# A recurrence with its inverse as products on quarters of the array, fewer half writes, six banks, and queues issued in a listed order

## The chip, the core and the metric

One core of a Trainium2 chip runs the whole program. The metric is the device time of one execution in microseconds (us), the median of several. The engines are TensorE (PE, with its weight loads as PEld), VectorE (DVE), ScalarE (ACT), GpSimd (POOL) and SyncE (SP), which issues the DMAs.

## What is computed

Two transformer blocks in sequence over 512 tokens of 1024 features, in float32 with a context of 256 tokens. The part that matters here is the scan of the second layer of the first block, over 16 heads of 64 features, in two directions, first over the context and then over the tokens:

```python
def step(S, inp):
    w_t, k_t, v_t, kk_t, kka_t = inp[:5]
    S = (S * w_t[:, :, None, :]
         - jnp.einsum('bhij,bhj->bhi', S, kk_t)[..., None] * kka_t[:, :, None, :]
         + v_t[..., None] * k_t[:, :, None, :])
    y = jnp.einsum('bhij,bhj->bhi', S, inp[5]) if emit else None
    return S, y
```

The decay `w_t` comes from a bias, `w0`, and a low-rank product, through a sigmoid and an exponential. What is read out of the scan (`rwkv_readout`) is normalised by head, given a bonus term and a gate, and multiplied by a weight.

## The kernel before

The kernel computes the scan in chunks of 64 tokens. `wkv` makes 24 cells, 3 rounds of 8: round `b` is the context for 0 and a half of the tokens for 1 and 2, and `p` is a pair of heads; both directions `d` of 4 chunks each are in one cell, so a tile of [128, 8, 64] holds 2 heads on the partitions and 8 chunks. Cell i needs the state `H` that cell i-8 left.

`cell` (line 1225) loads k, kk, r, the low-rank weights l2 and w0 (spread over 128 partitions on the host); forms the decay from T1 and l2 in PSUM, adds w0 on DVE, takes the Tanh on ACT; sums the decays with a triangular product (tri) and exponentiates them to W and iW; writes BC (each head's two operands side by side, so in halves of 64 partitions, on DVE and POOL), AQ and Qz. `intra` (line 1340) makes the scores of 64 by 64 tokens (SC), and inverts a triangular matrix per chunk and head: three levels and a correction, 18 products that depend on each other, each copied out of PSUM by ACT (`cp`) or masked by DVE. Its left operands MB, ML and GT lie in zeroed tiles `bd`, [128, 8, 2, 64] float16, with the two heads' blocks on the diagonal, so `bdm` is 8 products of 128 by 128 on the whole array:

```python
for e in range(8):
    mm(ps[:, e], L[:, e].rearrange("p h t -> p (h t)"), x[:, e], start=first and e == 0, stop=last and e == 7)
```

`plus` adds a tile by one product of 512 columns with an identity, and `tr` transposes with 16 products on quarters (64 by 64, one per head). Because of the zeros, what DVE writes into GT is written in two halves. `step` (line 1450), four times a cell, is the scan over chunks: X from SC and HV, copied to Xs by ACT; U from TTz and Xs, copied into HV, one half by ACT and one by DVE; HU from the identity, BCt and HV, scaled by DVE into the next HV; for the tokens also Q, added into ytm. `readout` (line 1512) normalises a pair of heads after round 2, with DVE, ACT and POOL.

PSUM has 4 banks `ps` for the inverse and the scores and 4 `ch` for the steps. At most three cells hold the tiles SC, BCt, TTz and HV. What sets the order: the cells and readouts are generators, which `Clock.weave` (line 96) runs by turns, each to its next yield, the lowest cell first among those that an estimate of the engines' times finds ready; signals such as ("chain", i - 3) keep a cell from starting early. The instructions so traced go to a scheduler behind it, which sorts each engine's queue by its own estimates. On the chip each queue is worked off in order. Every operation goes through one helper, so the profile shows line 176 for all of them; the tile names tell them apart (`bd` for MB, ML and GT, `f` for the float16 copies, `c_...` for constants).

Of the kernel before, what the change touches and what calls it, by code (L numbers as in the profile page):

```python
# [14 lines left out]
PSUM = bass.MemoryType.PSUM  # L15

P = 128
D = 1024
KD = 8
# [6 lines left out]
class Clock:  # L26
# [5 lines left out]
    def __init__(self):  # L32
        self.free, self.wrote, self.used = {}, {}, {}
        self.now = self.end = 0.0
        self.events = {}
        self.fresh = []
        self.taken = self.given = 0
        self.tiled = False

# [95 lines left out]

def _cost(eng, fn, out, ins, tiled=False):
    n = _size(out)
    if eng == "PE":
        if tiled and ins[0].dtype == F32 and min(ins[0].shape[0], _size(ins[0])) <= 64:

            return 0.5 * (0.00085 if fn == "transpose" else 0.0017) * max(n, 60)
# [12 lines left out]


class Engine:
# [5 lines left out]
    def __getattr__(self, fn):  # L162
        real, clock, eng = getattr(self._r, fn), self._c, self._n

        def call(*a, **k):
            aps = [x for x in list(a) + list(k.values()) if isinstance(x, bass.AP)]
            out = k.get("out", a[0] if a else None)
            ins = [x for x in aps if x is not out]
            outs = [out.tensor.name]
            if "accum_out" in k:  # L170
                outs.append(k["accum_out"].tensor.name)
            if eng == "DMA":
                clock.dma(outs[0], [x.tensor.name for x in ins], out.shape[0] * _size(out) * 4)
            else:
                clock.op(eng, _cost(eng, fn, out, ins, clock.tiled), outs, [x.tensor.name for x in ins])
            return real(*a, **k)  # L176

        setattr(self, fn, call)
        return call


# [7 lines left out]
class Core:  # L189
# [54 lines left out]
    def ring(self, pool, shape, tag, bufs, dt=F32):  # L244

        t = pool.tile(shape, dt, name=self.nm(tag), tag=tag, bufs=bufs)
        r = self.rings.setdefault((id(pool), tag), [])
        r.append(t.tensor.name)
        if len(r) > bufs:
            self.clock.follow(r[-1], r[-1 - bufs])  # L250
# [248 lines left out]
class First:  # L499
# [691 lines left out]
    def wkv(self, dr, ytm, bonus):  # L1191
# [3 lines left out]
        v, s, g = nc.vector, nc.scalar, nc.gpsimd  # L1195
        es = c.psums(ps=4, ch=4)
        c.clock.tiled = True
        self.op = pool = es.enter_context(c.tc.tile_pool(reuse_waits="tile", name="wkv", bufs=1))
        for n in ("id16", "a0", "ka", "rk", "scmask", "lvl", "tri", "i16", "iq", "hsel"):
            setattr(self, n, self.load_in(pool, n))  # L1200
# [18 lines left out]
        c.clock.tiled = False  # L1219
        es.close()  # L1220
# [4 lines left out]
    def cell(self, i, b, p, dr, ytm, bonus):  # L1225
# [32 lines left out]
        for j in range(2):  # L1258
            for d in range(2):
                mm(ps[d][:, j * P:(j + 1) * P], self.T1[rr[d], qd[d] * 256 + j * P:qd[d] * 256 + (j + 1) * P], l2[rr[d], :P], start=j == 0, stop=False)  # L1260
        for d in range(2):
            mm(ps[d][:, 256:], l2[rr[d], P:], self.A1[rr[d], tok[d]], start=False, stop=True)
        for d in range(2):
# [3 lines left out]
        yield  # L1267
        s.activation(sw, sw, AF.Tanh, scale=0.5)
        yield
# [19 lines left out]
        yield  # L1289
        BC, AQ = self.wt([8, 2, 64], "BC"), self.wt([8, 2, 64], "AQ")  # L1290
        v.scalar_tensor_tensor(th8, th8, 1.0, kk8, op0=ALU.add, op1=ALU.mult)
        for h in range(2):

            rr = np.s_[h * 64:(h + 1) * 64]
            v.scalar_tensor_tensor(BC[rr, :, h], th8[rr], 0.5, iW[rr], op0=ALU.mult, op1=ALU.mult)
            g.tensor_tensor(BC[rr, :, 1 - h], kd[rr], iW[rr], op=ALU.mult)
        a = AQ[:, :, 0]
# [42 lines left out]
    def intra(self, i, out, BC, AQ):  # L1340
# [9 lines left out]
        bc = lambda h, e: BC[hs[h], e].rearrange("p o s -> p (o s)")  # L1350
        SC = []
        for d in range(2):
            sc = self.wt([2, 4, P], "SC", 6)
            ps = [c.psum().rearrange("p (c t) -> p c t", c=4) for _ in range(2)]
            for ch in range(4):
                for h in range(2):
                    mm(ps[h][:, ch, :nq], bc(h, d * 4 + ch), AQ[hs[h], d * 4 + ch].rearrange("p o s -> p (o s)")[:, :nq], start=ch == 0, stop=ch == 3)
            for h in range(2):
                v.tensor_tensor(sc[:, h, :, :nq], ps[h][:, :, :nq], self.scmask[:, d, :nq].unsqueeze(1).to_broadcast([P, 4, nq]), op=ALU.mult)
                m = sc[hs[h], h, :, :64]  # L1360
                s.copy(MB[hs[h], d * 4:(d + 1) * 4, h], m)
                (g, v)[h].tensor_tensor(ML[hs[h], d * 4:(d + 1) * 4, h], m, MB[hs[h], d * 4:(d + 1) * 4, h], op=ALU.subtract)
                g.tensor_copy(m, AQ[hs[h], d * 4:(d + 1) * 4, 0])
# [3 lines left out]
        for e in range(8):  # L1367
            for h in range(2):
                nc.tensor.transpose(pt[h][:, e], bc(h, e), c.ident[hs[h], hs[h]])
        for h in range(2):  # L1370
            s.copy(BCt[:, :, h], pt[h])
# [78 lines left out]
    def step(self, p, qd, st, SC, BCt, TT, Qz, HV, wc, ytm):  # L1450
# [15 lines left out]
        s.copy(Xs, X)  # L1466
        HU = half()
        for d, h in DH:
            mm(HU[hs[h], d], c.ident[:, hs[h]], HV[:, es[d], h], start=d == 0, stop=False)
        if out:  # L1470

            Q = half()
            for h, d in DH:
                mm(Q[hs[d], h], Qz[:, es[d], h], HV[:, es[d], h], start=h == 0, stop=False)
        yield
# [6 lines left out]
        for d, h in DH:  # L1482
            mm(HU[hs[h], d], BCt[:, es[d], h], HV[:, es[d], h], start=False, stop=d == 1)
        if st < 3:
# [4 lines left out]
        if out:  # L1489
            for h, d in DH:  # L1490
                mm(Q[hs[d], h], SC[d][:, h, chs[d], 64:128], HV[:, es[d], h], start=False, stop=h == 1)
            for d in range(2):
# [19 lines left out]
    def readout(self, p, dr, y, bonus, ring, G1):  # L1512
# [19 lines left out]
        yield ("chain", 2 * KD + p)  # L1532
        sm = c.tmp.tile([P, 8], F32, name=c.nm("gs"), tag="gs")
        v.reduce_sum(sm, e8(y), axis=X1)
# [8 lines left out]
        yield  # L1543
        vr = c.tmp.tile([P, 8], F32, name=c.nm("gv"), tag="gv")
        v.reduce_sum(vr, e8(t), axis=X1)
# [10 lines left out]
        for j in range(4):  # L1556
            nc.tensor.transpose(pt[:, j * P:(j + 1) * P], y[:, j * P:(j + 1) * P], c.ident)
        s.copy(y, pt)
        yield
        ps = c.psum()  # L1560
        c.mm3(ps, (wh, wl), np.s_[:, :], G1, np.s_[:, :], True, True)
        v.tensor_tensor(y, y, ps, op=ALU.mult)
# [1057 lines left out]
```

## Time and profile before

| | |
|---|---|
| median of 3 runs | 4526.43 us (4525.61 to 4526.72) |
| profiled execution | 4529.56 us |
| its span, first to last instruction | 4527.8 us |
| mean granted clock of TensorE | 0.945 |
| busy in the span | PE 4146.5, DVE 2583.0, ACT 1747.0, POOL 1150.1 us |

The span is what the profile divides up; the time of the execution has 1.8 us more around it. A busy PE counts an instruction from its start to its modelled end, and consecutive products overlap. [...]

### The profile page before, as it was taken

What the parts mean: (1) busy time and instruction counts of PE and PEld (TensorE: products, weight loads), DVE (VectorE), ACT (ScalarE), POOL (GpSimd) and SP (SyncE); (2) the same over time, 40 slices, a digit from 0 to 9 for tenths busy, and PEclk for the clock granted to TensorE, in tenths of its full rate; (3) what the DMA queues carried; (4) which work ended last, traced back from release to release, by engine and by line L of the source; (5) the groups of instructions that cost most, each with busy time, mean ns of one, the idle gap of its engine ahead of it and who ended that gap; (6) DMA issues with size and microseconds to landing.
All of it is one profiled execution on the core that took longest, in us unless ns stands there. A gap on an engine that the chain in (4) does not pass through costs nothing. (4 is left out here: it accounts for less than half of the span.)

```text
span 4527.8 us, 69045 instructions
## 1 busy us (share of the span) xinstructions
PE 4146.5 (92%) x27872; PEld 3436.0 (76%) x27872; DVE 2583.0 (57%) x4105; ACT 1747.0 (39%) x3265; POOL 1150.1 (25%) x1122
## 2 busy tenths in 40 slices
PE   5897899997897988887999999988999999979998
PEld 4786688886685777766888788876888888857887
DVE  8998844345934666677644543486433433584333
ACT  4454422223534556544522432225322322334222
POOL 4223300003514344453200211163201201353111
PEclk8898999999898899988999999998999999979999
DMA  6444421212233111112432322220332323211332
GB/s 220 148 134 134 148 75 62 65 63 96 84 122 102 42 46 52 47 40 63 137 107 94 98 95 97 93 76 18 103 98 94 97 96 96 93 38 62 97 98 84
DMA packets 193889, 408.80 MB, mean 90 GB/s; under 512 B 46496, under 2 KB 87456, under 8 KB 193568
## 3 DMA queue, kind: packets, MB, share of 16 engines
q1 hardware_dynamic: 193568, 404.37, 27.8%
q8 instruction: 219, 3.59, 0.3%
q14 instruction: 102, 0.84, 0.1%
HBM read 386.47 MB, written 17.83 MB: 89 GB/s over the span
## 5 line engine op out<-in xcount | busy, mean ns | idle before, releaser
L176 PE MATMUL pj<-a,wh 128*128 128x512 f32 (+1 forms) x5328 | 1420.2, 356 | 73.7 <-DVE a L176 32.2
L176 PE MATMUL ps<-a,wh 128*128 128x512 f32 x4192 | 1293.4, 390 | 12.0 <-DVE a L176 6.4
L176 ACT CAST wh<-wr 128x1024 fp32r<-128x1024 f32 (+3 forms) x548 | 565.2, 1031 | 1643.9 <-PE ps L176 952.6
L176 PEld LDWEIGHTS pj<-a,wh 128*128 128x128 f32 x5328 | 951.6, 195 | 221.8 <-issue 43.7
L176 PE MATMUL pj<-a,wl 128*128 128x512 f32 (+1 forms) x2664 | 939.2, 353 | 26.5 <-DVE wl L176 20.5
L176 PEld LDWEIGHTS ps<-a,wh 128*128 128x128 f32 x4192 | 786.5, 188 | 176.9 <-DVE a L176 7.5
L176 PE MATMUL ps<-a,wl 128*128 128x512 f32 x2096 | 815.5, 389 | 0.0
L176 DVE TENSOR_TENSOR wl<-wr,wh 128x1024 fp32r<-128x1024 f32 (+3 forms) x490 | 599.1, 1223 | 301.9 <-ACT wh L176 269.7
L176 PEld LDWEIGHTS pj<-a,wl 128*128 128x128 f32 x2664 | 517.9, 195 | 102.2 <-DVE wl L176 26.7
L176 PEld LDWEIGHTS ps<-a,wl 128*128 128x128 f32 x2096 | 393.8, 188 | 81.8
L176 POOL TENSOR_TENSOR t<-t,a 128x512 f32<-128x512 f32 x94 | 159.6, 1699 | 1113.4 <-ACT t L176 1113.4
L176 POOL TENSOR_TENSOR a<-a,t 128x512 f32<-128x512 f32 (+1 forms) x109 | 142.1, 1306 | 1023.0 <-ACT t L176 1021.6
L176 PE MATMUL ps<-a,a 128*128 128x256 f32 (+4 forms) x859 | 195.7, 383 | 35.4 <-ACT a L176 15.1
L176 ACT CAST f<-ps 128x512 f16<-128x512 f32 x312 | 178.0, 587 | 119.9 <-PE ps L176 117.9
L176 DVE SCALAR_TENSOR_TENSOR ytm<-ps,ytm 128x512 f32<-128x512 f32 x96 | 66.4, 692 | 264.9 <-PE ps L176 264.9
L176 DVE TENSOR_TENSOR t<-t,ps 128x512 f32<-128x512 f32 x87 | 59.8, 688 | 275.2 <-PE ps L176 270.6
L176 DVE TENSOR_TENSOR a<-a,pj 128x512 f32<-128x512 f32 (+1 forms) x176 | 101.2, 578 | 166.9 <-PE pj L176 166.9
L176 PEld LDWEIGHTS <-bd 128*128 128x128 f16 x3264 | 139.8, 102 | 72.3 <-issue 24.7
L176 PEld LDWEIGHTS ps<-a,a 128*128 128x128 f32 (+1 forms) x859 | 136.2, 212 | 73.0 <-ACT a L176 24.3
L176 POOL TENSOR_TENSOR wl<-wr,wh 128x1024 fp32r<-128x1024 f32 x58 | 150.8, 2605 | 148.1 <-ACT wh L176 126.2
L176 DVE TENSOR_TENSOR t<-ps,a 128x512 f32<-128x512 f32 x86 | 59.2, 691 | 220.5 <-PE ps L176 220.5
L176 DVE SCALAR_TENSOR_TENSOR a<-a,c_cvw,a 128x511 f32<-128x511 f32 (+15 forms) x180 | 177.7, 1007 | 2.3
(301 smaller groups left out, 5557.7 us busy)
## 6 DMA issues: line engine op xcount, KB each, us to landing
wr<-in_f1w SPq DMA_DIRECT2D x120, 512.0 KB, 3.5
wr<-in_f2w SPq DMA_DIRECT2D x120, 512.0 KB, 3.5
ada<-in_adaT SPq DMA_DIRECT2D x88, 512.0 KB, 3.6
wr<-in_m0w SPq DMA_DIRECT2D x76, 512.0 KB, 3.6
wr<-in_m1w SPq DMA_DIRECT2D x76, 512.0 KB, 3.6
wr<-in_ev_o SPq DMA_DIRECT2D x16, 512.0 KB, 3.9
wr<-in_w_o SPq DMA_DIRECT2D x16, 512.0 KB, 3.5
k<-d_k SPq DMA_DIRECT2D x48, 128.0 KB, 2.2
```

The source lines that it names most:

```text
L176: return real(*a, **k)
```

## The change

The three masked operands become dense tiles of [128, 8, 64], and each whole-array product becomes two products on quarters, one per head; `plus` likewise. GT and RT are written once for all 128 partitions, and BC gets a layout with k's operand in the middle, shared by both heads' reads, so that POOL writes it once. w0 is loaded as one row per direction into a zeroed tile and added by a product with a tile `first`, which has ones in one row per direction, and ACT takes the Tanh from PSUM. The banks become 6 `ps`, 1 `ch` (X and U) and 1 `hq` (HU and Q). The generators are run one after the other into a `Plan`, which keeps every instruction as a step (consecutive PE instructions of a cell are one step), and lists them by a greedy simulation with a price for each and room for each ring of tiles; the four engines' queues then follow that list.

```diff
@@ Engine.__getattr__ @@
+            if clock.plan is not None:
+                return clock.plan.add(eng, fn, lambda: real(*a, **k), out, ins, outs)
@@ new: class Step (one instruction, or a group of PE's) @@
+    def product(self, fn, out, ins):
+        k, m, n = ins[0].shape[0], _size(ins[0]), _size(out)
...
+        mode = k > 64, m > 64
+        if self.mode is None:
+            self.first = mode
+        elif mode != self.mode:
+            self.at = self.cost + 0.1
...
+        once = max(0.00084 * n, 0.054) if plain else 0.00042 * n + 0.003
...
@@ new: class Plan @@
+    LAT = 0.2
+    def add(self, eng, fn, call, out, ins, outs):
+        st = self.steps[-1] if self.steps else None
+        if not (st and eng == st.eng == "PE" and st.rank[0] == self.rank):
+            st = Step(eng, outs[0], (self.rank, len(self.steps)))
+            self.steps.append(st)
...
+            if eng == "ACT":
+                st.cost = 0.17 + 0.00082 * n
+            elif eng == "DVE":
+                st.cost = 0.16 + 0.00105 * n
+            elif fn == "tensor_tensor":
+                st.cost = 0.2 + 0.0024 * n
+            else:
+                st.cost = 0.18 + 0.0009 * n
...
+    def order(self):
...
+                    t = max(f + (self.SWITCH if eng == "PE" and steps[i].first != mode else 0.0), ready[i])
+                    need = {}
+                    for x in uses[i]:
+                        if x not in held:
+                            need[self.place[x]] = need.get(self.place[x], 0) + 1
+                    for k, n in need.items():
+                        if len(room[k]) < n:
+                            break
+                        t = max(t, sorted(room[k])[n - 1] + 0.1)
+                    else:
+                        at[i] = t
...
+                lo = min(at.values())
+                i = min((x for x in at if at[x] <= lo + self.SLACK), key=lambda x: steps[x].rank)
+                if best is None or at[i] < best[0]:
+                    best = at[i], i
...
+        return [steps[i] for _, i in sorted(out)]
+    SWITCH = 0.1
+    SLACK = 0.1
@@ wkv @@
-        es = c.psums(ps=4, ch=4)
+        es = c.psums(ps=6, ch=1, hq=1)
...
-        self.bd = [[zero(pool.tile([P, 8, 2, 64], F16, name=c.nm("bd"))) for _ in range(3)] for _ in range(3)]
-        cells = [self.cell(i, i // KD, i % KD, dr, ytm, bonus) for i in range(3 * KD)]
+        self.w0z = [zero(pool.tile([P, P], F32, name=c.nm("w0z"))) for _ in range(3)]
+        self.first = zero(pool.tile([P, P], F32, name="first"))
...
-        c.clock.weave(cells + [self.readout(p, dr, ytm[p], bonus, ring, self.G1) for p in range(KD - 1)])
+        plan = c.clock.plan = Plan()
+        for i in range(3 * KD):
+            plan.rank = i
+            run(self.cell(i, i // KD, i % KD, dr, ytm, bonus))
+            if i >= 2 * KD and i < 3 * KD - 1:
+                plan.rank = i + 1.5
+                run(self.readout(i - 2 * KD, dr, ytm[i - 2 * KD], bonus, ring, self.G1))
+        c.clock.plan = None
+        with c.tc.manual_schedule(engines={E.PE, E.Activation, E.DVE, E.Pool}):
+            for step in plan.order():
+                for call in step.calls:
+                    call()
@@ cell @@
-        w0 = self.wt([2, P], "w0")
-        nc.sync.dma_start(w0, c.A["w0r"][:, :, p * P:(p + 1) * P])
+        w0 = self.w0z[i % 3]
+        for d in range(2):
+            nc.sync.dma_start(w0[d * 64:d * 64 + 1], c.A["w0r"][0:1, d, p * P:(p + 1) * P])
...
+        for j in range(2):
+            for d in range(2):
+                mm(ps[d][:, j * P:(j + 1) * P], self.first[rr[d]], w0[rr[d]], start=False, stop=False)
...
-            v.tensor_tensor(sw[:, 2 * d:2 * d + 2], ps[d][:, :256].rearrange("p (j f) -> p j f", j=2),
-                            w0[:, d].unsqueeze(1).to_broadcast([P, 2, P]), op=ALU.add)
+            s.activation(sw[:, 2 * d:2 * d + 2], ps[d][:, :256].rearrange("p (j f) -> p j f", j=2), AF.Tanh, scale=0.5)
...
-        s.activation(sw, sw, AF.Tanh, scale=0.5)
...
-            g.tensor_tensor(BC[rr, :, 1 - h], kd[rr], iW[rr], op=ALU.mult)
+        g.tensor_tensor(BC[:, :, 1], kd, iW, op=ALU.mult)
@@ intra @@
-        MB, ML, GT = self.bd[i % 3]
+        MB, ML, GT = (self.wt([8, 64], n, 3, F16) for n in ("MB", "ML", "GT"))
...
-                mm(ps[:, e], L[:, e].rearrange("p h t -> p (h t)"), x[:, e], start=first and e == 0, stop=last and e == 7)
+                for h in range(2):
+                    mm(ps[hs[h], e], L[hs[h], e], x[hs[h], e], start=first and e == 0, stop=last and e == 7)
...
-            mm(ps.rearrange("p e t -> p (e t)"), self.id16, x.rearrange("p e t -> p (e t)"), start=True, stop=False)
+            for h in range(2):
+                mm(ps[hs[h]].rearrange("p e t -> p (e t)"), self.i16[hs[h]], x[hs[h]].rearrange("p e t -> p (e t)"), start=True, stop=False)
...
-            for h in range(2):
-                v.tensor_tensor(GT[hs[h], :, h].rearrange("p (d c) t -> p d c t", d=2), ps[hs[h]].rearrange("p (d c) t -> p d c t", d=2),
-                                self.lvl[hs[h], l].unsqueeze(2).to_broadcast([64, 2, 4, 64]), op=ALU.mult)
+            v.tensor_tensor(GT.rearrange("p (d c) t -> p d c t", d=2), ps.rearrange("p (d c) t -> p d c t", d=2),
+                            self.lvl[:, l].unsqueeze(2).to_broadcast([P, 2, 4, 64]), op=ALU.mult)
...
-        for h in range(2):
-            v.tensor_tensor(RT[hs[h], :, h], iq[hs[h]], ps[hs[h]], op=ALU.subtract)
+        v.tensor_tensor(RT, iq, ps, op=ALU.subtract)
@@ step @@
-        HU = half()
+        HQ = c.bank("hq", (P, 2, 2, 64))
+        HU, Q = HQ[:, 0], HQ[:, 1]
```

The readouts' small tiles become rings of two, and its gate products are issued before ACT's copy.

## Rows read from the trace of the kernel before

**Rows 1.** Stretches: us, busy PE PEld DVE ACT POOL (count), clock, DMA share, GB/s.

```profile
1406.00:2128.00 722.00, 621.28 (x10513) 506.44 (x10513) 491.12 (x950) 403.56 (x925) 314.55 (x451) 0.89 0.17 47
1660.00:1880.00 220.00, 195.02 (x3677) 159.90 (x3676) 151.10 (x288) 140.72 (x344) 96.88 (x141) 0.96 0.17 48
1880.00:2110.00 230.00, 195.31 (x3173) 159.63 (x3173) 166.45 (x332) 108.39 (x242) 106.21 (x129) 0.84 0.13 36
```

**Rows 2.** The same view, middle stretch, instructions on H alone (DVE, POOL).

```profile
1660.00:1880.00 220.00, 2.33 (x8) 4.60 (x16) 0.96 0.17 48
```

**Rows 3.** Waits of PE in the recurrence: us in total, times, longest.

```profile
PE ch L176 <- DVE hv L176: 29.3, 24, 3.6
```

**Rows 4.** Timeline of DVE: start, us, what; idle before and what ended it.

```profile
2094.57 0.69 DVE L176 TENSOR_TENSOR ytm<-ytm,gv 128x512 f32<-128x512 f32 x1 [1.76 <-POOL gv L176]
2095.30 1.39 DVE L176 TENSOR_TENSOR bd<-ps,c_lvl 64x512 f16<-64x512 f32 x2
2096.72 0.69 DVE L176 TENSOR_TENSOR ytm<-ytm,ps 128x512 f32<-128x512 f32 x1
2097.44 0.29 DVE L176 COPY hv<-ch 64x128 f32<-64x128 f32 x1
```

**Rows 5.** Two stretches, one at each clock (columns as in the first group).

```profile
1444.00:1491.00 47.00, 39.36 (x770) 31.31 (x766) 30.56 (x56) 31.39 (x69) 16.05 (x28) 1.00 0.12 32
1492.00:1502.00 10.00, 9.94 (x110) 8.49 (x111) 6.45 (x13) 3.73 (x10) 1.54 (x3) 0.51 0.13 38
```

**Rows 6.** The same stretches, PE's whole-array products (those that read bd) alone.

```profile
1444.00:1491.00 47.00, 15.49 (x328) 1.00 0.12 32
1492.00:1502.00 10.00, 1.67 (x24) 0.51 0.13 38
```

**Rows 7.** Timeline of PE at the upper clock.

```profile
1673.27 1.61 PE L176 MATMUL ps<-AQ,BC 64*128 64x128 f32 x16
1674.80 0.45 PE L176 MATMUL ch<-Xs,TTz 128*64 128x64 f32 x8
...
1680.42 0.40 PE L176 MATMUL ch<-hv,c_ident 128*64 128x64 f32 x8
1680.65 0.40 PE L176 MATMUL ch<-hv,Qz 128*64 128x64 f32 x8
1680.98 0.44 PE L176 MATMUL ps<-c_i,f 64*64 64x64 f16 x16
1681.35 0.45 PE L176 MATMUL ch<-Xs,TTz 128*64 128x64 f32 x8
1681.73 0.39 PE L176 MATMUL ps<-c_iq,c_id 128*128 128x512 f16 x1
1681.96 0.40 PE L176 MATMUL ps<-c_iq,bd 128*128 128x64 f16 x8
1682.19 0.38 PE L176 MATMUL ps<-f,c_id 128*128 128x512 f16 x1
```

**Rows 8.** Timeline of PE at the lower clock.

```profile
1492.06 0.60 PE L176 MATMUL ps<-c_i,f 64*64 64x64 f16 x16 [0.92 <-ACT f L176]
1492.59 1.97 PE L176 MATMUL ps<-AQ,BC 64*128 64x64 f32 x16
...
1500.24 0.70 PE L176 MATMUL ch<-Xs,TTz 128*64 128x64 f32 x8
1500.87 1.87 PE L176 MATMUL ps<-c_tri,sw 128*128 128x128 f32 x8
```

**Rows 9.** Groups by form, recurrence: count, busy us, mean ns, idle before.

```profile
L176 DVE TENSOR_TENSOR bd<-ps,c_lvl 64x512 f16<-64x512 f32 x144 | 99.1, 688 | 21.1 <-PE ps L176 18.2
L176 POOL TENSOR_TENSOR BC<-kd,iW 64x512 f32<-64x512 f32 x48 | 70.7, 1473 | 1.9
L176 DVE TENSOR_TENSOR bd<-c_iq,ps 64x512 f16<-64x512 f16 x48 | 32.9, 685 | 10.6 <-PE ps L176 9.7
L176 DVE TENSOR_TENSOR sw<-ps,w 128x256 f32<-128x256 f32 x48 | 18.1, 420 | 21.8 <-PE ps L176 21.2
```

More of the change, by code (lines that the diff above doesn't have):

```diff
@@ L133, in _size, with _cost @@
     return n
-def _cost(eng, fn, out, ins, tiled=False):
+def _cost(eng, fn, out, ins):
     n = _size(out)
     if eng == "PE":
-        if tiled and ins[0].dtype == F32 and min(ins[0].shape[0], _size(ins[0])) <= 64:
-            return 0.5 * (0.00085 if fn == "transpose" else 0.0017) * max(n, 60)
         if fn == "transpose":
@@ L174, in call @@
             else:
-                clock.op(eng, _cost(eng, fn, out, ins, clock.tiled), outs, [x.tensor.name for x in ins])
+                clock.op(eng, _cost(eng, fn, out, ins), outs, [x.tensor.name for x in ins])
             return real(*a, **k)
@@ L179, in __getattr__, with __init__ @@
         return call
+class Step:
+    def __init__(self, eng, key, rank):
+        self.eng, self.key, self.rank = eng, key, rank
+        self.calls, self.deps, self.next = [], set(), []
+        self.cost, self.mode, self.first = 0.0, None, None
+        self.array, self.at = {}, 0.0
+    def product(self, fn, out, ins):
+        k, m, n = ins[0].shape[0], _size(ins[0]), _size(out)
+        rows = (0, 1) if k > 64 else (int(ins[0].start_partition() >= 64),)
+        cols = (0, 1) if m > 64 else (int(out.start_partition() >= 64),)
+        part = [(r, x) for r in rows for x in cols]
+        mode = k > 64, m > 64
[3 more added lines that the diff above has]
+            self.at = self.cost + 0.1
+        self.mode = mode
+        plain = ins[0].dtype == F32
+        once = max(0.00084 * n, 0.054) if plain else 0.00042 * n + 0.003
+        at = max([self.at] + [self.array.get(p, 0.0) for p in part])
+        fin = at + once * (2 if plain and fn != "transpose" else 1)
+        for p in part:
+            self.array[p] = fin
+        self.at = at + 0.006
+        self.cost = max(self.cost, fin)
@@ new lines, with __init__, claim @@
+class Plan:
+    LAT = 0.2
+    def __init__(self):
+        self.steps, self.rank = [], 0
+        self.writer, self.readers, self.touch = {}, {}, {}
+        self.place, self.room = {}, {}
+    def add(self, eng, fn, call, out, ins, outs):
[3 more added lines that the diff above has]
+            self.steps.append(st)
+        i = len(self.steps) - 1
+        st.calls.append(call)
+        for x in ins:
+            t = x.tensor.name
+            if t in self.writer:
+                st.deps.add(self.writer[t])
+            self.readers.setdefault(t, set()).add(i)
+            self.touch.setdefault(t, set()).add(i)
+        for t in outs:
+            if t in self.writer:
+                st.deps.add(self.writer[t])
+            st.deps |= self.readers.get(t, set())
+            self.readers[t] = set()
+            self.writer[t] = i
+            self.touch.setdefault(t, set()).add(i)
+        st.deps.discard(i)
+        if eng == "PE":
+            st.product(fn, out, ins)
+        elif eng == "DMA":
+            st.cost = 0.1 + out.shape[0] * _size(out) * 4 / 270e3
+        else:
+            n = _size(out if fn != "reduce_sum" else ins[0])
+            if eng == "ACT":
[6 more added lines that the diff above has]
+                st.cost = 0.18 + 0.0009 * n
+    def claim(self, *tiles):
+        for t in tiles:
+            self.touch.setdefault(t.tensor.name, set()).add(len(self.steps) - 1)
+    def order(self):
+        steps = self.steps
+        left, ready, free, fin = [], [0.0] * len(steps), {}, [0.0] * len(steps)
+        for i, s in enumerate(steps):
+            left.append(len(s.deps))
+            for d in s.deps:
+                steps[d].next.append(i)
+        rest = {t: len(x) for t, x in self.touch.items() if t in self.place}
+        last = dict.fromkeys(rest, 0.0)
+        uses = [[] for _ in steps]
+        for t in rest:
+            for i in self.touch[t]:
+                uses[i].append(t)
+        held, room = set(), {k: [0.0] * n for k, n in self.room.items()}
+        can = {}
+        for i, s in enumerate(steps):
+            can.setdefault(s.eng, set())
+            if not left[i]:
+                can[s.eng].add(i)
+        mode, out = None, []
+        while any(can.values()):
+            best = None
+            for eng, c in can.items():
+                if not c:
+                    continue
+                f = free.get(eng, 0.0)
+                at = {}
+                for i in c:
+                    t = max(f + (self.SWITCH if eng == "PE" and steps[i].first != mode else 0.0), ready[i])
[7 more added lines that the diff above has]
+                        t = max(t, sorted(room[k])[n - 1] + 0.1)
+                    else:
+                        at[i] = t
+                if not at:
+                    continue
+                lo = min(at.values())
+                i = min((x for x in at if at[x] <= lo + self.SLACK), key=lambda x: steps[x].rank)
+                if best is None or at[i] < best[0]:
+                    best = at[i], i
+            if best is None:
+                break
+            at, i = best
+            s = steps[i]
+            for x in uses[i]:
+                if x not in held:
+                    held.add(x)
+                    places = room[self.place[x]]
+                    places.remove(min(places))
+            can[s.eng].remove(i)
+            if s.eng == "PE":
+                mode = s.mode
+            free[s.eng] = at + s.cost
+            fin[i] = at + s.cost + (2.0 if s.eng == "DMA" else 0.0)
+            out.append((at, i))
+            for x in uses[i]:
+                rest[x] -= 1
+                last[x] = max(last[x], fin[i])
+                if not rest[x]:
+                    room[self.place[x]].append(last[x])
+            for j in s.next:
+                lat = self.LAT if steps[j].eng != s.eng else 0.0 if s.eng == "PE" else 0.06
+                ready[j] = max(ready[j], fin[i] + lat)
+                left[j] -= 1
+                if not left[j]:
+                    can[steps[j].eng].add(j)
+        assert len(out) == len(steps), (len(out), len(steps))
+        self.time = max(fin)
+        return [steps[i] for _, i in sorted(out)]
+    SWITCH = 0.1
+    SLACK = 0.1
@@ L248, in ring @@
         r.append(t.tensor.name)
+        if self.clock.plan is not None:
+            self.clock.plan.place[t.tensor.name] = id(pool), tag
+            self.clock.plan.room[id(pool), tag] = bufs
         if len(r) > bufs:
@@ L1214, in wkv @@
         self.TTz = [zero(pool.tile([P, 8, 2, 64], F32, name=c.nm("TTz"))) for _ in range(3)]
-        self.bd = [[zero(pool.tile([P, 8, 2, 64], F16, name=c.nm("bd"))) for _ in range(3)] for _ in range(3)]
-        cells = [self.cell(i, i // KD, i % KD, dr, ytm, bonus) for i in range(3 * KD)]
+        self.w0z = [zero(pool.tile([P, P], F32, name=c.nm("w0z"))) for _ in range(3)]
+        self.first = zero(pool.tile([P, P], F32, name="first"))
+        for d in range(2):
+            g.memset(self.first[d * 64:d * 64 + 1], 1.0)
         ring = lambda n, tag, dt=F32: c.ring(self.rp, [P, n], tag, 1, dt)
-        c.clock.weave(cells + [self.readout(p, dr, ytm[p], bonus, ring, self.G1) for p in range(KD - 1)])
-        c.clock.tiled = False
+        plan = c.clock.plan = Plan()
[10 more added lines that the diff above has]
+                    call()
+        c.clock.now += plan.time
+        for e in c.clock.free:
+            c.clock.free[e] = c.clock.now
         es.close()
@@ L1369, in intra @@
                 nc.tensor.transpose(pt[h][:, e], bc(h, e), c.ident[hs[h], hs[h]])
+        c.clock.plan.claim(BCt)
         for h in range(2):
@@ L1470, in step @@
         if out:
-            Q = half()
             for h, d in DH:
-                mm(Q[hs[d], h], Qz[:, es[d], h], HV[:, es[d], h], start=h == 0, stop=False)
+                mm(Q[hs[d], h], Qz[:, es[d], h], HV[:, es[d], h], start=False, stop=False)
         yield
@@ L1482, in step @@
         for d, h in DH:
-            mm(HU[hs[h], d], BCt[:, es[d], h], HV[:, es[d], h], start=False, stop=d == 1)
+            mm(HU[hs[h], d], BCt[:, es[d], h], HV[:, es[d], h], start=False, stop=d == 1 and not out)
+        if out:
+            for h, d in DH:
+                mm(Q[hs[d], h], SC[d][:, h, chs[d], 64:128], HV[:, es[d], h], start=False, stop=h == 1)
         if st < 3:
```

30 lines of the change are left out of this document (15 added, 15 removed).

## The prediction

> **What bounds the kernel now.** The change touches one stretch alone, the recurrence, so first I looked for where it lies: from the first product with T1 to the last update of H, 1406 to 2128 us, 722 us of the span. The table by stretches gives its engines [rows 1]. No engine is full: PE 621 us busy, DVE 491, ACT 404, POOL 315, DMA at 0.17. The middle stretch holds the updates of H of 8 cells in 220 us, so a cell takes 27.5 us there [rows 2]; over all 24 cells it is 30.1. PE, the busiest, stands still for 101 us. The longest of its waits is for DVE's hv, 29.3 us [rows 3], and one place shows how that comes about: DVE first waits 1.76 us for POOL's gv of a readout, then writes two halves of GT (bd, 1.39 us) and a readout product, and only then, at 2097.44, copies the half of hv for which the next products of another cell's step are waiting [rows 4]. The queues run in order, so a step waits behind work that is not urgent. What I read: the recurrence is held up by the order of its queues and by latencies, with PE next in line, and the clock of PE on top.
>
> **The clock.** [...] From 1492 to 1502 us PE was busy for 9.94 of 10 us, and the clock was 0.51; from 1444 to 1491 it was busy for 39.4 of 47 us, and the clock was 1.00 [rows 5]. What differs is the work: 24 products on the whole array in the former (2.4 per us), 328 in the latter (7 per us) [rows 6]. The change removes just these products, which is my reason for doubt.
>
> **What PE has to do.** At the upper level I take the time from a run's start to the next run's start, not its busy time, whose end is modelled. 8 whole-array products take 0.23 us, one of 512 columns 0.23, 16 quarter products 0.37 with a change of shape behind them, 8 products with c_ident 0.23, 8 with Qz 0.33 with a change: a change of shape costs 0.10. 16 score products take 1.53 with a change [rows 7]. A cell's inverse has 17 runs of 8 whole products, 8 of 512 columns and 3 of 16 quarters: 17 x 0.23 + 8 x 0.23 + 3 x 0.27 = 6.5 us. Its four steps have 24 runs of some 0.26: 6.2 (16 runs, 4.2, in a context cell). The scores take 3.1 (2 in a context cell, where they are half as wide), and the decay, gate and bonus products and the transposes, priced at the same rate, about 4 (3). Some 27 changes of shape, one per us as around 1681, give 2.7. That is 22.5 us, and 18.4 in a context cell: 16 x 22.5 + 8 x 18.4 = 507, with the readouts 515 us. At the lower level the same runs take longer: 16 quarters 0.53 against 0.37, 8 with TTz 0.63 against 0.38 [rows 7, 8], so it works at 0.60 to 0.70 of the upper rate; I take 0.62, nearer to the step products, which are many. [...]
>
> **Part by part.**
> - Quarters: 17 runs of 8 become runs of 16. With the change behind it the run takes 0.37 against 0.23 + 0.10: +0.04 each, +0.7 us a cell. The 8 of 512 columns become pairs that can run side by side; bounds 0 and +0.23 each, and I take 0, since 16 quarters in 0.27 are already less than twice 8 wholes. The transposes no longer change the shape before and behind: -0.6. [...]
> - w0 as products: 8 instructions of the scores' form, half of 1.53: +0.77 us of PE a cell. DVE loses two additions of 0.42 a cell, 18 us in all [rows 9]. ACT's Tanh reads PSUM in two pieces, and DVE's step between PE and ACT is gone. One load of 128 KB becomes two of one row; SP has one issue more, and DMA at 0.17 hides it. If that cover were gone, the start of a cell, two cells ahead, would be late.
> - Half writes: GT and RT are written once for 128 partitions in place of twice for 64. Of 99.1 + 32.9 us [rows 9] half goes, since an instruction's time goes by its columns: DVE -66 us, and 0.69 off four hops of each inverse. POOL loses half of BC's 70.7 us, off the path: POOL is at 315 of 722. Its nine memsets of bd lie before the start, which waits for the loads of the first cell. They are worth nothing.
> - So DVE falls to 491 - 84 = 407 us, and PE has 515 + 24 x 0.9 = 536 us to do. PE is the engine that bounds.
> - Six banks: the inverse and the scores get 6 for 4. X and U now share one bank, which costs nothing, as U needs X's copy anyway. HU and Q share one for a whole step, so two cells' steps can't lie side by side. There are 96 steps; the 32 of the middle stretch's 8 cells in 220 us are 6.9 us each. Were they to stay that long and stand in line, they alone would take 660 us. They must get shorter, by the next part.
> - The listed order: four engines issue as listed, one PE group of a cell as a whole, the oldest cell first among what can start within 0.1 us. Where this helps is such a place [rows 4]: hv should come ahead of GT. What then is late is PE itself. A listed queue also adds waits where the list's prices are off: behind a late readout product on DVE stand the same hv copies, and PE behind them. The loads stay with SP's own queue, which is not listed.
>
> **The sum.** With u for what PE does outside the lower level and f for the lower level's share, the recurrence takes 536 / (u (1 - f) + 0.62 f). For u the bounds are 0.74 (order no better) and 1; I take 0.88, a quarter of the way from the best stretch's 0.84 to 1, since each cell's inverse still has 18 products in a chain, between which PE must be filled from only three cells. For f the bounds are 0.08 (clock 0.96, middle stretch) and 0.98 (the stretch from 1492); I take 0.32, that of the third stretch at 0.84 [rows 1]: it is the lowest clock that lasted over several cells, and so the row nearest to the new mix. 536 / (0.598 + 0.198) = 673 us: **49 us less**. The profiled execution took 4529.56 us (span 4527.8), so 4480; it is 3 us above the median of 4526.43, so **4477**. With u from 0.84 to 0.92 and f from 0.2 to 0.45 this case runs from 4425 to 4520.
>
> **The rivals.**
> - *The clock stays up.* PE is fuller, so f is 0.05: 536 / (0.836 + 0.031) = 618, 104 us less, 4422; for u of 0.92 it is 4400. For it: the middle stretch, the densest, has 0.96. Against it: full PE at 0.51 [rows 5]. [...] Chance 0.13.
> - *The order brings nothing.* The queues were sorted by estimated times before as well, and three cells' buffers (BCt, TTz, hv) are unchanged. u is 0.80, f 0.32: 722, no change, 4526. For it: the change does not do what it says if the waits are latencies. Against it: the wait there is one of order [rows 4]. Chance 0.14.
> - *The quarters lower the clock.* [...] It decides from where 0.88 - 0.26 f falls below 0.742, f = 0.53, a clock of 0.74. For it: what differs between the two clocks [rows 5, 6]. Against it: a faster pace has more of every kind of work per us. Chance 0.21.
>
> **How the numbers follow.** The forecast keeps 0.52. Within 0.2%, 9 us, is about what a measurement of this kernel can tell from no change. Faster: 0.50 of the forecast, 0.13 of the first rival, 0.02 of the second: 0.65. Same: 0.02 and 0.08: 0.10. Slower: 0.21 and 0.04: 0.25. The range reaches from 4405, inside the first rival, to 4570, inside the third, and leaves out about 2 in 10.
>
> **What would show it.** Right: a recurrence of some 670 us; DVE busy about 407 us in it, with GT and RT written by 96 instructions of 128 partitions; 16 quarters still in 0.27 to 0.37; PE's wait for hv well below 29; a clock between 0.80 and 0.88. The forecast is wrong if the clock is below 0.74 or near 0.96, if 16 quarters take 0.5 or more, if steps still take 7 us, or if the time moves outside the recurrence.

## The result, and the profile after

The kernel after takes 4447.12 us, the median of 4 runs (4443.47 to 4450.39), against 4526.58 for the kernel before on the same chip: a ratio of **0.9824, with an interval of 0.9807 to 0.9841**, 79.5 us less. The forecast was 4477: the sign and the range held, the gain was put 30 us too low.

The table by stretches of the kernel after, from the first product with T1 to the last update of H and then by its three rounds of 8 cells (columns as in [rows 1]):

```profile
1401.00:2050.00 649.00, 586.39 (x14162) 493.21 (x14162) 395.31 (x808) 412.52 (x952) 272.94 (x430) 0.92 0.18 49
1401.00:1644.00 243.00, 218.25 (x5012) 183.45 (x5014) 139.70 (x266) 158.58 (x357) 98.13 (x173) 0.90 0.21 59
1644.00:1851.00 207.00, 192.91 (x4822) 164.24 (x4815) 114.68 (x233) 141.36 (x346) 81.77 (x135) 0.93 0.16 45
1851.00:2050.00 199.00, 175.23 (x4344) 145.52 (x4340) 140.93 (x310) 112.58 (x250) 93.04 (x124) 0.94 0.16 42
```

The same view of the kernel before, by the same rounds:

```profile
1406.00:1668.00 262.00, 225.15 (x3578) 182.89 (x3578) 165.69 (x312) 152.13 (x332) 106.18 (x174) 0.87 0.20 54
1668.00:1884.00 216.00, 190.41 (x3611) 156.57 (x3608) 153.08 (x288) 137.69 (x338) 100.81 (x143) 0.97 0.18 50
1884.00:2128.00 244.00, 205.73 (x3330) 166.99 (x3329) 172.35 (x351) 113.74 (x255) 107.56 (x135) 0.84 0.13 35
```

The recurrence fell from 722 to 649 us, and the clock in it rose from 0.89 to 0.92. The rounds lost 19, 9 and 45 us: most went in the third, where the readouts run beside the cells, and where the place of [rows 4] lies. PE's time without work in the stretch (its length less PE's busy time) fell from 101 to 63 us, and its busy time by 35, though it has more instructions to do. In the profiled executions the start came 5 us earlier and what follows the recurrence was 8 us shorter; the variants below scatter by about as much in both, so neither is put down to the change.

Waits of PE in the recurrence, after (columns as in [rows 3]):

```profile
PE ps L171 <- DMA l<-in_l: 12.6, 1, 12.6
PE ps L171 <- ACT f L171: 11.6, 28, 1.3
PE ps L171 <- DVE th L171: 11.1, 12, 2.9
PE ps L171 <- DVE GT L171: 8.7, 9, 2.1
PE ps L171 <- DVE sw L171: 8.0, 6, 2.9
PE hq L171 <- DVE hv L171: 5.1, 7, 1.5
PE ch L171 <- DVE hv L171: 4.3, 14, 0.7
```

The wait for DVE's hv, 29.3 us into `ch` before [rows 3], is 4.3 there and 5.1 into `hq`: 9.4 in all. The first line, the wait for the loads of the first cell, ends with the first product, where the stretch begins, so it is no part of the 63 us; the longest in the stretch is now that for ACT's f.

The groups of the recurrence that answer to [rows 9]:

```profile
L171 DVE TENSOR_TENSOR GT<-ps,c_lvl 128x512 f16<-128x512 f32 x72 | 49.5, 689 | 18.5 <-PE ps L171 17.4
L171 POOL TENSOR_TENSOR BC<-kd,iW 128x512 f32<-128x512 f32 x24 | 33.4, 1393 | 11.8 <-PE ps L171 11.7
L171 ACT ACTIVATE sw<-ps 128x256 f32<-128x256 f32 x48 | 18.5, 386 | 33.8 <-PE ps L171 33.6
L171 DVE TENSOR_TENSOR GT<-c_iq,ps 128x512 f16<-128x512 f16 x24 | 16.5, 687 | 16.9 <-PE ps L171 16.7
```

GT and RT take 49.5 + 16.5 = 66.0 us where they took 99.1 + 32.9 = 132: here a write of 128 partitions took as long as one of 64 did (689 and 687 ns against 688 and 685). BC's first operand fell from 70.7 to 33.4 us on POOL. The Tanh from PSUM took the place of DVE's 18.1 us of additions.

PE's timeline at the upper clock, after (columns as in [rows 7]):

```profile
1700.93 0.40 PE L171 MATMUL ps<-f,c_i 64*64 64x512 f16 x2
1701.17 0.41 PE L171 MATMUL ps<-f,GT 64*64 64x64 f16 x16
1701.51 0.45 PE L171 MATMUL hq<-hv,BCt 128*64 128x64 f32 x8
...
1708.64 0.71 PE L171 MATMUL ps<-l,T1s 64*128 64x128 f32 x8
1709.18 0.61 PE L171 MATMUL ps<-w0z,first 64*128 64x128 f32 x8
1709.63 0.60 PE L171 MATMUL ps<-A1s,l 64*128 64x256 f32 x4
```

From start to start, two products of 512 columns on quarters take 0.24 us, 16 quarter products 0.34 with a change of shape behind them, and the eight with w0 0.45.

### The profile page after: what moved, and what is told of

It is laid out like the page before. It is cut to its first block, busy times and chain, and to the rows that moved or that the text cites. A ratio compares the mean times of both kernels' runs of the same rounds, so it can differ in the third digit from the quotient of the medians.

```text
span 4441.7 us, 76269 instructions
## 1 busy us (share of the span) xinstructions
PE 4102.2 (92%) x31520; PEld 3414.6 (77%) x31520; DVE 2478.7 (56%) x3961; ACT 1754.9 (40%) x3289; POOL 1097.0 (25%) x1095
## 3 DMA queue, kind: packets, MB, share of 16 engines
q1 hardware_dynamic: 186992, 401.22, 29.3%
## 5 line engine op out<-in xcount | busy, mean ns | idle before, releaser
L176 ACT CAST a<-t 128x512 fp32r<-128x512 f32 (+1 forms) x206 | 116.3, 565 | 115.5 <-DVE t L176 115.2
```

## The experiments

The theory was that **the order** does it (the list, with which the scheduler behind the weave is also switched off for the four engines; no run parts these two): the list lets urgent work go first on each engine, and PE then works closer to its limit. The rival was that **the parts** do it, the 84 us taken off DVE above all; and against both stood the rival of the prediction that **quarters** lower the clock. Every variant computes the whole of the reference. In the table, the recurrence is taken as above, "without work" is its length less PE's busy time, and the ratio is against the kernel before on the same chip.

| kernel | queues | banks ps/ch/hq | median us | ratio (interval) | recurrence us | clock | PE without work |
|---|---|---|---|---|---|---|---|
| before | woven | 4/4 | 4526.6 | 1 | 722 | 0.89 | 101 |
| after | listed | 6/1/1 | 4447.1 | 0.9824 (0.9807 to 0.9841) | 649 | 0.92 | 63 |
| e1 | woven | 6/1/1 | 4575.8 | 1.011 (1.0092 to 1.0128) | 777 | 0.85 | 103 |
| e2, old products | listed | 4/4 | 4482.8 | 0.9912 (0.9895 to 0.9928) | 682 | 0.91 | 100 |
| e3, whole-array | listed | 6/1/1 | 4453.5 | 0.984 (0.9825 to 0.9855) | 655 | 0.92 | 76 |
| e4 | listed | 4/2/2 | 4466.3 | 0.9872 (0.9857 to 0.9887) | 665 | 0.92 | 71 |
| e5 | woven | 4/2/2 | 4515.5 | 0.9975 (0.9963 to 0.9988) | 715 | 0.90 | 94 |
| e6, old products | woven | 6/1/1 | 4541.4 | 1.0036 (1.0024 to 1.0047) | 736 | 0.90 | 111 |
| e7, two half writes | listed | 6/1/1 | 4474.1 | 0.988 (0.9863 to 0.9897) | 676 | 0.91 | 76 |
| e8, list tuned | listed | 6/1/1 | 4418.4 | 0.9752 (0.9734 to 0.977) | 612 | 0.96 | 46 |
| e9, w0 on DVE | listed | 6/1/1 | 4436.7 | 0.9801 (0.9785 to 0.9817) | 634 | 0.92 | 59 |
| e10, wider window | listed | 6/1/1 | 4428.5 | 0.9777 (0.9762 to 0.9791) | 627 | 0.95 | 53 |
| e11, measured prices | listed | 6/1/1 | 4395.3 | 0.9708 (0.9694 to 0.9723) | 591 | 0.97 | 34 |
| e12, e11 and w0 on DVE | listed | 6/1/1 | 4389.7 | 0.970 (0.9683 to 0.9717) | 591 | 0.96 | 38 |

The kernels ran on several chips, on which the kernel before took 4523.9 to 4529.0 us, so a difference of medians below can be off by some 5 us; where it matters, the ratios decide.

**All but the list.** The generators are woven as before; the weave prices products of 64 x 64 at half.

```diff
-        plan = c.clock.plan = Plan()
...
+        c.clock.weave(cells + [self.readout(p, dr, ytm[p], bonus, ring, self.G1) for p in range(KD - 1)])
```

> Everything of the change but the listed order: the cells and readouts go through the turns of before again, with quarters priced by their concurrency; banks 6, 1 and 1. If the order carries the gain, this loses most of the 79 us: 4505 to 4535 us, with PE's waits in the recurrence near 100 us. If the shorter hops of the inverse carry it, 4450 to 4480 us, with PE's waits near 63.

Measured: 4575.8 us, 49 more than before and 129 more than after, above both ranges. PE's waits in its recurrence begin so:

```profile
PE ps L182 <- ACT f L182: 33.0, 44, 6.5
PE hq L182 <- DVE hv L182: 23.2, 16, 4.4
PE ps L182 <- DVE GT L182: 20.3, 20, 3.2
```

DVE has 407 us of work here and POOL 284, nearly as in the kernel after, and yet the time is above that of before: less work on these engines does not by itself make the recurrence shorter. The wait for hv, 23.2 us into `hq` and 1.9 into `ch`, is not far below that of [rows 3]. What the banks have to do with this comes further down.

**The list alone.** Plan and order on the products, half writes, w0, BC and banks of before (the small changes to the readouts stay).

```diff
+        plan = c.clock.plan = Plan()
+        for i in range(3 * KD):
+            plan.rank = i
+            run(self.cell(i, i // KD, i % KD, dr, ytm, bonus))
...
-        c.clock.weave(cells + [self.readout(p, dr, ytm[p], bonus, ring, self.G1) for p in range(KD - 1)])
```

> The listed order alone on the products, half writes, w0 addition and banks (4 and 4) of before. If the order carries the gain: 4450 to 4480 us. If it needs the other parts: 4495 to 4525 us. The clock tells a third thing: if whole-array products hold it up, it is above the changed kernel's 0.92 in the recurrence.

Measured: 4482.8 us, 44 less than before, with DVE still at 480 us of work. More than half of the gain is the list's alone. But PE is without work for as long as before: the wait for hv fell by more than half, and the one for ACT's f grew. The first line is of the kernel before, the others of e2:

```profile
PE ps L176 <- ACT f L176: 18.4, 38, 1.6
PE ps L171 <- ACT f L171: 29.3, 60, 2.4
PE ch L171 <- DVE hv L171: 13.1, 19, 2.1
```

So the first half of the theory, that urgent work goes first, shows here in hv alone; what the recurrence loses is busy time of PE, of which more below.

**Whole-array products in the kernel after**, and with them the half writes that they need.

```diff
-                for h in range(2):
-                    mm(ps[hs[h], e], L[hs[h], e], x[hs[h], e], start=first and e == 0, stop=last and e == 7)
+                mm(ps[:, e], L[:, e].rearrange("p h t -> p (h t)"), x[:, e], start=first and e == 0, stop=last and e == 7)
```

> The changed kernel with the inverse as products on the whole array again, so that GT and RT are written in halves again; order, banks and w0 product stay. If quarters cost clock and PE time, as forecast, this is faster in PE and DVE's 66 us are hidden: 4400 to 4440 us and a clock above 0.92. If DVE's halves lie on the chain: 4460 to 4500 us.

Measured: 4453.5 us, between the two ranges, 6 more than after, with intervals that overlap: what quarters and single writes bring together isn't told from nothing. Its recurrence, in the columns used above:

```profile
1401.00:2056.00 655.00, 578.75 (x10706) 475.96 (x10706) 447.66 (x903) 411.01 (x952) 267.09 (x430) 0.92 0.17 48
```

The clock is 0.92 with whole-array products and 0.92 with quarters. The rival "quarters lower the clock" falls, at this pace.

**Banks.** First the kernel after with `es = c.psums(ps=4, ch=2, hq=2)`, so that two steps can lie side by side:

> The changed kernel with 4 banks for the inverse and the scores, 2 for X and U and 2 for HU and Q. If six banks matter: 4460 to 4500 us. If one bank for a whole step holds the steps up more: 4420 to 4440 us. If neither: within 9 us of 4447.

Then the woven one of the first experiment with the same banks:

> As the run without the list (4576 us), but with 4 banks for the inverse and the scores, 2 for X and U and 2 for HU and Q, so that two cells' steps can lie side by side again. If the single bank for a whole step made that run slower than before: 4490 to 4530 us. If quarters at a slow pace did, by PE's clock: 4560 to 4590 us with a clock near 0.85 in the recurrence.

And the kernel before with six banks and the step that shares one:

> The kernel before with banks 6, 1 and 1 alone, in the old order, with products on the whole array. If the single bank for a whole step costs in the old order: 4550 to 4600 us, near the run without the list. If it does not, and quarters cost there: 4500 to 4530 us.

Measured: under the list, 4/2/2 costs 19 us (4466.3 against 4447.1). Under the weave it is the other way round: 4515.5 against 4575.8, so there the single bank per step costs 60 us, and 15 on the kernel before (4541.4, below the range named for that). What the six banks are worth depends on the order. The fourth and fifth also give the list's worth with all else the same: 4466.3 against 4515.5, 49 us; of the 50 by which the recurrences differ, 23 are time without work on PE and 27 its busy time. And the fifth gives the other parts' worth without the list: 11 us.

**The half writes by themselves.** The kernel after, quarters kept, with GT and RT each written in two halves:

```diff
-            v.tensor_tensor(GT.rearrange("p (d c) t -> p d c t", d=2), ps.rearrange("p (d c) t -> p d c t", d=2),
...
+            for h in range(2):
+                v.tensor_tensor(GT[hs[h]].rearrange("p (d c) t -> p d c t", d=2), ps[hs[h]].rearrange("p (d c) t -> p d c t", d=2),
```

> The changed kernel with GT and RT written in two halves of 64 partitions again, on quarters all the same. If the half writes are what the inverse gains by: 4465 to 4490 us, DVE busy 66 us longer. If DVE's work is hidden now: within 9 us of 4447.

Measured: 4474.1 us. Its recurrence:

```profile
1400.00:2075.00 675.00, 599.41 (x14162) 500.42 (x14160) 451.77 (x902) 413.61 (x952) 264.54 (x430) 0.91 0.17 47
```

So single writes are worth 27 us (25 by the ratios), and quarters with the same half writes cost 21 (4474.1 against 4453.5; 18 by the ratios): PE is busy for 599.4 us with quarters and 578.8 with whole products. The quarters are a price paid so that the writes can be single.

**The list's window, its prices and w0.** Three kernels: a wider window for the oldest cell alone (e10); the same window with readouts ranked two cells later and POOL's pow on 8 columns priced as the trace has it (e8); the kernel after with w0 added by DVE as before (e9). The edits to the list:

```diff
-    SLACK = 0.1
+    SLACK = 0.28
...
-                st.cost = 0.2 + 0.0024 * n
+                st.cost = 1.7 if n <= 8 else 0.2 + 0.0024 * n
...
-                plan.rank = i + 1.5
+                plan.rank = i + 3.5
```

> The changed kernel with one number of the list changed: candidates within 0.28 us, in place of 0.1, are taken by age. If that is what the tuned list (4418 us) gained by: 4415 to 4430 us. If it was the price of the power operation or the place of the readouts: within 9 us of 4447.

> The changed kernel with another list: POOL's small power operation priced at the 1.7 us that the trace shows, candidates within 0.28 us in place of 0.1 taken by age, and readouts ranked two cells later. If the order still holds something: 4425 to 4440 us. If what is left is PE's work and clock: within 9 us of 4447.

> The changed kernel with w0 added by DVE again, loaded spread over 128 partitions, one Tanh on ACT after it. If PE's work bounds the recurrence, the 18 us of PE that this takes away show: 4425 to 4440 us. If the hop of DVE between PE and ACT lies on the chain: 4455 to 4475. If neither: within 9 us of 4447.

Measured: the window alone 4428.5 us, 19 less than after; with new prices and ranks besides 4418.4, 10 less again, but the intervals of these two overlap. w0 on DVE gave 4436.7, 10 less than after; the intervals just overlap, so that w0 as products costs time is likely and not shown. For it speaks that PE is busy for 574.9 us there, 11 less, at the same clock.

**Prices as measured.** The tuned list (e8) with the hop from one engine to the next, the floor of a product with 128 weight columns and second buffers (for kd and sw too), and a window of 0.217 us in place of 0.28:

```diff
-                lat = self.LAT if steps[j].eng != s.eng else 0.0 if s.eng == "PE" else 0.06
+                lat = (0.21 if s.eng == "PE" else 0.07) if steps[j].eng != s.eng else 0.0 if s.eng == "PE" else 0.04
...
-        once = max(0.00084 * n, 0.054) if plain else 0.00042 * n + 0.003
+        once = max(0.00084 * n, 0.115 if m > 64 else 0.054) if plain else 0.00042 * n + 0.003
...
-        W, iW = self.wt([8, 64], "W", 1), self.wt([8, 64], "iW", 1)
+        W, iW = self.wt([8, 64], "W", 2), self.wt([8, 64], "iW", 2)
```

> The tuned list with prices from the traces: 0.21 us from PE to another engine and 0.07 between others, in place of 0.2; 0.115 us for a pass of a product with 128 columns of weights in float32; candidates within 0.217 us by age; two buffers for W, iW, kd and sw. If wrong prices in the list still cost: 4395 to 4412 us. If not: within 9 us of the tuned list's 4418.

> The list with measured prices (4395 us), with w0 added by DVE again and candidates within 0.25 us by age. If PE's work still bounds, the 18 us of PE taken away show in part: 4378 to 4388 us. If the order had been what w0 cost (a new list for fewer steps): within 9 us of 4395.

Measured: 4395.3 us, and 4389.7 with w0 on DVE and a window of 0.25. The two intervals overlap; both lie below that of the kernel after. The recurrence of the former:

```profile
1403.00:1994.00 591.00, 557.13 (x14162) 471.05 (x14160) 384.34 (x807) 412.75 (x952) 267.01 (x430) 0.97 0.20 54
```

These are the products of the kernel after, in 58 us less: 29 us fewer without work on PE and 29 fewer of PE's busy time, at a higher clock. Which of the edits in it brings how much wasn't taken apart.

## Why the prediction was right, and where it was off

**What bounds: right.** The wait of one order on DVE was the place to look at [rows 4]: the wait for hv fell by 20 us with the change, to 9.4, where e1 without the list has 25.1. That a queue is worked off in order shows at another place of the kernel before: ACT copied its half of an hv at 2100.70, out of the product that DVE's half comes from too, but DVE stood idle for 2.41 us, up to 2101.90, until the load of vv, and copied its half only behind the addition to vv, at 2102.63. The rival "the order brings nothing" falls with e2. But e2 shows too that less waiting for hv isn't less waiting: PE's time without work is 101 us before, 100 with the list alone and 94 with the other parts alone (e5), and falls to 63 to 76 only where the list and other parts come together.

**DVE's work: right in its main term.** GT and RT lost 66.0 us, as forecast; DVE came to 395 us where 407 were forecast, for a reason told in the last section. But this work isn't beside the path: single writes bring 27 us under the list (e7). The prediction named the 0.69 us that they take off four hops of each inverse, and gave them no price of their own in the sum.

**PE's work: right by the row, wrong in two terms.** Quarters were put at 0.7 us a cell, 17 in all, and 0.6 a cell, 14 in all, was taken off again because the transposes would no longer change the shape. e7 against e3 shows 21 us of PE's busy time, where these two terms leave 2 or 3. The saving wasn't there: counted as told below, e7 has 644 changes of shape in the recurrence and e3 664, so 20 fewer where 6 a cell would have been 144; at 0.10 each, 12 us weren't saved. The pairs of 512 columns were taken at 0 and take 0.24 against 0.23 for one whole [rows 7]. w0 takes 0.45 us a cell and not 0.77, 11 us in all: 8 us of PE's work less than in the sum. That these two errors nearly cancel is luck.

**Banks: right that steps had to get shorter.** The 60 us by which e1 lies above e5 are what the prediction said of steps that stand in line. Under the list six banks gain 19, so the single bank no longer costs more than it gives. That steps got shorter isn't measured: by the prediction's own count, a round over its 32 steps, it is 207 / 32 = 6.5 us in the second round after, where 6.9 was read before.

**The clock: the step that failed.** The term that was mis-sized is f, the share of the time at the lower level. It was put at 0.32, after the third stretch's 0.84 [rows 1], "the row nearest to the new mix"; the clock was 0.92, and the traces of before and after have it at 1.00 or at 0.50 and nowhere between, so f was 0.08 / 0.50 = 0.16. With the measured 649 us and the 536 of work, u is 0.866, since 0.866 x 0.84 + 0.62 x 0.16 = 0.826 and 536 / 0.826 = 649; 0.88 was forecast. No run shows the 0.74 and the 0.84 on which that 0.88 rests; an estimate of the former from the trace of before is that the 158 us at the lower level hold 98 us of the 515 of work, at the rate of 0.62, and the other 564 us the remaining 417, which is 0.74. With the 8 and the 12 us of the paragraph on PE's work it is 0.87. So u was nearly right, and a little high; with f of 0.32 the same u gives 681 us, and the 32 us between are the whole miss in the recurrence and more. What was wrong in f is the reason for it: the 0.84 was read as a mark of the mix of products. The runs don't bear that out. The same instructions had 0.85 in e1 at 777 us, 0.92 at 649 and 0.97 in e11 at 591, and with whole-array products it was 0.92 at 655: the clock went with the pace, not with the shape of the products. Nor did the prediction's own sign, a clock of 0.80 to 0.88, come. And no run shows a time for the rival "the quarters lower the clock", inside which the range ends at 4570: the lowest clock of a recurrence in the table is e1's 0.85.

What PE did before the clock fell shows where the reading of [rows 5] and [rows 6] went wrong. They compare the work inside a stretch at the lower level with that inside one at the upper. But the 10 us at 0.51 come right after 4 us at the upper level in which PE was busy for only 2.14, and a fall in the kernel after looks the same. The columns are us, PE's busy time (count), clock, DMA share and GB/s; the first two lines are of the kernel before, the others of the kernel after:

```profile
1488.00:1492.00 4.00, 2.14 (x39) 1.00 0.36 89
1492.00:1502.00 10.00, 9.94 (x110) 0.51 0.13 38
1549.00:1553.00 4.00, 1.71 (x52) 0.99 0.01 2
1553.00:1560.00 7.00, 7.00 (x98) 0.52 0.03 7
```

In the recurrences of the 14 kernels of the table, 191 falls to the lower level can be looked at in this way: in the 4 us before them PE was busy for 0.57 of the time on average, where it is busy for 0.84 to 0.94 of all the time at the upper level, by kernel; in the kernel before it is 0.54 for 22 falls against 0.85, in the kernel after 0.58 for 17 against 0.90. So in these traces the clock fell behind stretches with less work on PE, and a full PE inside a stretch at the lower level, where the same runs take longer (16 quarters 0.53 us against 0.37 [rows 7, 8]), says nothing of what brought the clock down. The time without work alone doesn't give the clock: it is 0.85 in e1 with 103 us, 0.91 in e2 with 100 and 0.90 in e6 with 111. The rival that the prediction held at 0.13 had a fuller PE keep the clock up; the order of events in these traces agrees with it, and the row from 1492, which was held against it, is no exception. With f of 0.16 the kernel after lies between that rival's 0.05 and the forecast's 0.32.

The sum has one slip besides: with u of 0.84 and f of 0.45 the first case reaches 4527, and not 4520.

**A term that the sum left out.** The prediction took some 27 changes of shape a cell, before as after. Counted along PE's timeline, a product whose shape differs from that of the one before it (in partitions or columns, up to 64 or above) comes 837 times in the recurrence before, 35 a cell, and 671 times after, 28 a cell; 651 times with the list alone, and 782 and 902 in the woven e5 and e1. At 0.10 each [rows 7], the 166 fewer are an estimated 17 us of PE's time. So the kernel before had some 19 us more to do than the 515 of the sum, and its u was 0.77 and not 0.74. The prediction called the gain a matter of waits and of fuller PE; part of it is that there are fewer changes of shape, for which the list has a price, and that it issues one cell's products as a group. e2 fits this: PE is without work as long as before, and the 40 us that the recurrence loses are all busy time. By estimate 19 of them are its 186 fewer changes, and 14 that it spends 121 us at the lower level in place of 158, at 0.62 of the rate. No run lists without that price or without the groups, so what each brings stays open; and fewer changes aren't all, since e11, among the fastest, has 691.

**Outside the recurrence** the forecast put nothing, and nothing there is shown to come from the change. The profiled execution after took 4443.47 us, the lowest of its four and 3.6 below their median; that of before lay 3 above its own.

## What to carry to other kernels

Where several chains share in-order queues, look in the waits for urgent work behind work that can wait, and list the queues before taking work off the engines: here the list was worth 44 to 129 us, by what it was put on, and the rest of the change without it 11 at best. A list can be tuned by the trace: with a wider window, other prices, ranks and second buffers the same instructions took 52 us less again, 19 of them by the window alone. Where the clock is low, look at what the engine did before it fell (here PE was busy for 0.57 of the 4 us before, on average), not at what it does while it is low. And judge an edit under the order it will run in: six banks cost 60 us under one order and gained 19 under the other.

## What the runs showed of the hardware that was not expected

Two kinds of DVE instruction with operands in SBUF, those that write th and BC, took much longer beside a POOL TENSOR_TENSOR: one that writes th 2.00 us against 0.75, those that write BC 1097 ns on average against 682. Two stretches of the kernel after, timelines of DVE and of POOL (start, us, what):

```profile
1574.94 2.00 DVE L171 SCALAR_TENSOR_TENSOR th<-kd,c_rk,r 128x512 f32<-128x512 f32 x1
...
1706.27 0.75 DVE L171 SCALAR_TENSOR_TENSOR th<-kd,c_rk,r 128x512 f32<-128x512 f32 x1
```

```profile
1575.13 1.26 POOL L171 TENSOR_TENSOR BC<-kd,iW 128x512 f32<-128x512 f32 x1
1576.35 1.71 POOL L171 TENSOR_TENSOR Qz<-W,r 64x512 f32<-64x512 f32 x1
...
1705.98 0.40 POOL L171 COPY SC<-AQ 64x256 f32<-64x256 f32 x1 [0.34 <-DVE ML L171]
1706.89 0.66 POOL L171 TENSOR_TENSOR ML<-SC,MB 64x256 f16<-64x256 f32 x1 [0.51 <-ACT MB L171]
```

The first, beside a POOL product of 1.26 us, took 1.25 us longer than the second, beside which POOL did little. Over all 48 instructions by which DVE writes its operand of BC in the kernel after, 64 x 512 each, the same shows: the 8 with no POOL instruction beside them took 682 ns on average, the 11 with nothing but POOL's copies 686, and the 29 with a POOL TENSOR_TENSOR 1097. The mean of all was 1150 ns before, 934 after and 792 in e11; the group in the kernel after:

```profile
L171 DVE SCALAR_TENSOR_TENSOR BC<-th,iW 64x512 f32<-64x512 f32 x48 | 44.8, 934 | 6.7 <-PE ps L171 4.9 <-ACT iW L171 1.2
```

So DVE's time in these runs went with what the order put beside it, and this covers the 12 us by which DVE fell below the forecast: 48 x (1150 - 934) ns are 10, and the 16 instructions that write th, with a mean of 1549 ns before and 1104 after, make 7 more. Why is not shown. The 1.25 us are about what that POOL product took, 1.26; but the DVE instruction is recorded as starting 0.19 us ahead of it, and POOL's copies, which read SBUF too, left DVE's instructions at 686 ns. No run was made to test it.
